# A two-block transformer kernel: expert slots weighted one at a time on ScalarE, choices in pieces, gathered rows also in the weight ring

## The chip, the core and the metric

The kernel runs on one core of a Trainium2 chip. The metric is the device time of one execution in microseconds (us); before is the median of three runs. Engines are named as the profile names them: PE (matmul), PEld (weight load), DVE (VectorE), ACT (ScalarE), POOL (GpSimd) and SP (which issues most loads).

## The reference

256 tokens of width 1024 pass through a first block (two layers of feed-forward, three attention-like branches and feed-forward) and a second block of two layers. Each layer of the second block is a mixer of five groups and then an expert layer, and only the expert layer is touched here:

```python
def peer_ffn(xn, wq, subkeys, u_tab, v_tab):
    q = (xn @ wq).reshape(b, s, PEER_HEADS, 2, PEER_HALF)
    sc = jnp.einsum('bshjc,hjkc->bshjk', q, subkeys)
    top_s, top_i = lax.top_k(sc, PEER_TOPK)
    ...                        # best 16 of the sums of both halves -> idx; g = softmax(best)
        act = jax.nn.gelu(jnp.einsum('ckd,cd->ck', u_tab[ic], xc), approximate=False)
        return jnp.einsum('ck,ckd->cd', (gc * act).astype(v_tab.dtype), v_tab[ic])
```

The table of experts has 16,384 rows per layer; a row holds u (1024 floats) and v (1024 floats) side by side, 8 KB. A token uses 8 x 16 = 128 of them, so a tile of 128 tokens needs 128 gathers ("slots"), each of 128 rows, 1 MB (1.049 million bytes); the two tiles of a layer need 256 slots, and both layers 512.

## The kernel before, in words

Everything is 32-bit. The first block and the mixers stream weights from memory through a ring of three 1 MB buffers (`raw`), which ACT and DVE (or POOL) split into a high and a low part (`hi` L212, `lo` L216) for three matmuls per product (`mm3`, L236). SP issues these loads as the ring comes free.

The expert layer is `peer`. `arrive` finishes a tile's input, `project(h)` computes the queries of a head (one 1 MB weight unit, 48 matmuls of L236) and the scores of its keys, and `route(tt, h)` chooses the 16 experts of a head on DVE (some 45 small instructions) and writes their numbers to `idx` and their softmax to `gate`. Then `experts` goes through the slots in groups of GROUP = 4:

- four times: POOL gathers a slot's rows into one of GBUFS = 8 buffers `uv` (L1377, an indirect DMA); DVE multiplies the u half with the token and sums it into one column of `act` (the "dot", L1379);
- once for the four: ACT takes Gelu of the 128x4 `act` (L1383), DVE multiplies it with the gates (L1384);
- four times: ACT scales the identity with one column (`dgw`, L1387), and PE multiplies that diagonal with the v half of the row (L1389: two halves of 512 columns, each recorded as two MATMULs), summing all 128 slots of a tile in `p_y`.

So a buffer `uv` is free for the next gather only when PE has read it, which is behind the dot of the last slot of its group.

What runs beside the slots is in `todo`: steps with the slot from which they may be issued. `issue_after(dots[-1])` ties a step behind the last dot of the group before; a whole `project` or `route` is one step. Tile 0 carries six projections, the second tile's arrival and the choices of its later heads, tile 1 the choices of its heads alone. The order of instructions within each engine is made at build time by a scheduler with a model of the time; the engines then run their lists in order, and semaphores hold them. Behind tile 0 the ring `raw` is free, and SP fills it with the first weights of the next mixer (`win2_s`); in the last layer it stays empty.

The changed function, with the line numbers of the profile:

Of the kernel before, what the change touches and what calls it, by code (L numbers as in the profile page):

```python
# [8 lines left out]
F32 = mybir.dt.float32  # L9
# [4 lines left out]
AF = mybir.ActivationFunctionType  # L14
OP = mybir.AluOpType
# [3 lines left out]
P = 128  # L19
T = 256  # L20
D = 1024
L = 2
NT = T // P
# [7 lines left out]
HEADS = 8  # L31
TOPK = 16
# [11 lines left out]
NEXP = NKEYS * NKEYS  # L44

GBUFS = 8
XG_AT = 3
GROUP = 4
NB2 = 17
LO = 4  # L50
BANKS = {"mm": 2, "acc": 4, "tr": 2}
# [124 lines left out]
class _Kernel:  # L176
# [1069 lines left out]
    def peer(self, l, x, xt, y_in):  # L1246
# [9 lines left out]
        def arrive(tt):  # L1256


            ss = self.small.tile([P, 2], F32, tag="rms_s", name="rms_s")
            r = rs[tt] = self.small.tile([P, 1], F32, tag="rms_r", name="rms_r", bufs=NT)  # L1260
            for i in range(2):
                sl = slice(512 * i, 512 * i + 512)
                nc.vector.tensor_tensor(x[tt][:, sl], y_in[tt][i], x[tt][:, sl], op=OP.add)
                nc.vector.tensor_tensor(xg[tt][:, sl], x[tt][:, sl], self.gain[:, sl], op=OP.mult)
                self.transposed(xg[tt][:, sl], KT // 2, xt, tt, k0=i * KT // 2)
            for i in range(2):
                sl = slice(512 * i, 512 * i + 512)
# [53 lines left out]
        def route(tt, h):  # L1321

            small = lambda n, t=F32, k=TOPK: W.tile([P, k], t, tag=n, name=n, bufs=2)
            sc = scores[tt, h]
            tv = W.tile([P, 2, TOPK], F32, tag="tv", name="tv", bufs=2)
            ti = W.tile([P, 2, TOPK], U32, tag="ti", name="ti", bufs=2)
            for j in range(2):
                top16(sc[:, j], tv[:, j], ti[:, j])

            c = W.tile([P, NPAIRS], F32, tag="cand", name="cand", bufs=2)  # L1330
            for a0, a1, w, at in PAIRS:
                nc.vector.tensor_tensor(c[:, at:at + (a1 - a0) * w].rearrange("p (a b) -> p a b", b=w),
                                        tv[:, 0, a0:a1].unsqueeze(2).to_broadcast([P, a1 - a0, w]),
                                        tv[:, 1, :w].unsqueeze(1).to_broadcast([P, a1 - a0, w]), op=OP.add)
            best, ci = small("best"), small("ci", U32)
            top16(c, best, ci)
            ids = W.tile([P, 2, TOPK], F32, tag="ids", name="ids", bufs=2)
            nc.vector.tensor_copy(ids, ti)

            cf, ai, ab, i1, i2 = small("cf"), small("ai", I32), small("ab"), small("i1"), small("i2")  # L1340
            nc.vector.tensor_copy(cf, ci)
            nc.vector.tensor_scalar(i1, cf, -11.5, 1.0 / 8.0, op0=OP.add, op1=OP.mult)
            nc.vector.tensor_scalar(i2, cf, -29.0, 1.0 / 3.0, op0=OP.add, op1=OP.mult)
            nc.vector.scalar_tensor_tensor(ai, i1, 0.0, i2, op0=OP.max, op1=OP.max)
            nc.vector.tensor_copy(ab, ai)
            nc.vector.tensor_scalar(i1, ab, 8.0, 8.0, op0=OP.mult, op1=OP.add)
            nc.vector.tensor_scalar(i2, ab, 3.0, 28.0, op0=OP.mult, op1=OP.add)
            nc.vector.scalar_tensor_tensor(i1, ab, 16.0, i1, op0=OP.mult, op1=OP.min)
            nc.vector.tensor_tensor(i1, i1, i2, op=OP.min)
            nc.vector.tensor_tensor(cf, cf, i1, op=OP.subtract)  # L1350
            for j, (pos, out) in enumerate(((ab, i1), (cf, i2))):
                e = W.tile([P, TOPK, TOPK], F32, tag="eq", name="eq", bufs=2)
                nc.vector.tensor_tensor(e, pos.unsqueeze(2).to_broadcast([P, TOPK, TOPK]),
                                        self.iota[:, :TOPK].unsqueeze(1).to_broadcast([P, TOPK, TOPK]), op=OP.is_equal)
                nc.vector.tensor_tensor(e, e, ids[:, j].unsqueeze(1).to_broadcast([P, TOPK, TOPK]), op=OP.mult)
                nc.vector.tensor_reduce(out, e, axis=AX.X, op=OP.add)
            nc.vector.scalar_tensor_tensor(i1, i1, float(NKEYS), i2, op0=OP.mult, op1=OP.add)
            last = nc.vector.tensor_scalar(idx[:, tt, h], i1, float(l * NEXP), None, op0=OP.add)
# [12 lines left out]
        def experts(tt, h, k0):

            rows = []
            act = W.tile([P, GROUP], F32, tag="act", name="act", bufs=3)
            for i in range(GROUP):
                r = uv.pop(0) if uv else W.tile([P, 2 * D], F32, tag="uv", name="uv", bufs=GBUFS)
                nc.gpsimd.indirect_dma_start(out=r, out_offset=None, in_=a["puv"],  # L1377
                                             in_offset=bass.IndirectOffsetOnAxis(ap=idx[:, tt, h, k0 + i:k0 + i + 1], axis=0))
                dots.append(nc.vector.scalar_tensor_tensor(r[:, :D], r[:, :D], 1.0, xg[tt], op0=OP.mult, op1=OP.mult,  # L1379
                                                           accum_out=act[:, i:i + 1]))  # L1380
                rows.append(r)
            wt = W.tile([P, GROUP], F32, tag="wt", name="wt", bufs=3)
            nc.scalar.activation(wt, act, AF.Gelu, scale=rs[tt])  # L1383
            nc.vector.tensor_tensor(wt, wt, gate[:, tt, h, k0:k0 + GROUP], op=OP.mult)  # L1384
            for i, r in enumerate(rows):
                dg = W.tile([P, P], F32, tag="dgw", name="dgw", bufs=4)
                nc.scalar.activation(dg, self.ident, AF.Copy, scale=wt[:, i:i + 1])  # L1387
                for half in range(2):
                    nc.tensor.matmul(y[tt][half], dg, r[:, D + 512 * half:D + 512 * half + 512],  # L1389
                                     start=h == 0 and k0 + i == 0, stop=h == HEADS - 1 and k0 + i == TOPK - 1)  # L1390


        weights(0)
        arrive(0)
        project(0, 0, 1)
        dots = [route(0, 0)]
        weights(1)
        project(1, 0, 1)

        def late():  # L1400
            arrive(1)
            if l + 1 < L:
                self.load_gain(l + 1)
            project(0, 1)
            project(1, 1)


        todo = [(0, lambda: route(0, 1)), (GROUP, late)]
        for h in range(2, HEADS):
            todo += [(TOPK * h - 22, lambda h=h: project(h)), (TOPK * h - 14, lambda h=h: route(0, h))]  # L1410
        for h in range(HEADS):
            todo.append((TOPK * (HEADS + h) - 24, lambda h=h: route(1, h)))
        todo.sort(key=lambda t: t[0])
        for n, (tt, h) in enumerate([(tt, h) for tt in range(NT) for h in range(HEADS)]):
            for k0 in range(0, TOPK, GROUP):
                while todo and todo[0][0] <= TOPK * n + k0:
                    step = todo.pop(0)[1]
                    with self.tc.issue_after(dots[-1].ins):
                        step()
                experts(tt, h, k0)  # L1420
        assert not todo
        return y

# [54 lines left out]
```

## Time and profile before

| | us |
|---|---|
| median of 3 runs (lowest, highest) | 3249.17 (3243.63, 3259.98) |
| the profiled execution | 3238.84 |
| its span, first to last instruction | 3237.1 |
| expert layer 0, first gather issued to last matmul | 1606.9 to 2347.7: 740.8 |
| expert layer 1, the same | 2515.0 to 3233.2: 718.2 |

The profile is of one execution; its span is 1.7 us under that execution's time, and that time 10.3 us under the median of the runs. A "stage" below is one tile of an expert layer; the four are 1606.9 to 1986, 1986 to 2347.7, 2515 to 2879 and 2879 to 3233.2 us. An engine's list is in order, so an idle time is read with what ended it (the text behind `<-`).

### The profile page before, as it was taken

What the parts mean: (1) busy time and instruction counts of PE and PEld (TensorE: products, weight loads), DVE (VectorE), ACT (ScalarE), POOL (GpSimd) and SP (SyncE); (2) the same over time, 40 slices, a digit from 0 to 9 for tenths busy, and PEclk for the clock granted to TensorE, in tenths of its full rate; (3) what the DMA queues carried; (4) which work ended last, traced back from release to release, by engine and by line L of the source; (5) the groups of instructions that cost most, each with busy time, mean ns of one, the idle gap of its engine ahead of it and who ended that gap; (6) DMA issues with size and microseconds to landing.
All of it is one profiled execution on the core that took longest, in us unless ns stands there. A gap on an engine that the chain in (4) does not pass through costs nothing.

```text
span 3237.1 us, 39712 instructions
## 1 busy us (share of the span) xinstructions
PE 2814.0 (87%) x13968; PEld 2058.1 (64%) x13968; DVE 2131.9 (66%) x4974; ACT 1199.3 (37%) x2300; POOL 882.7 (27%) x628
## 2 busy tenths in 40 slices
PE   9999999999999999999788877777889688867777
PEld 9988988989988988978644433332377344323333
DVE  6568667565577567569766676666487666766664
ACT  5446344445445344436432222212164322222121
POOL 0013221011023220011234454434311444444343
PEclk9999999999999999999889988888899899898889
DMA  6554235555553344554399999999843899999998
GB/s 256 183 187 158 100 122 202 183 182 213 182 189 135 105 156 176 182 184 144 129 379 397 391 371 365 397 378 374 344 146 108 347 391 376 378 399 384 379 376 353
DMA packets 121734, 841.78 MB, mean 260 GB/s; under 512 B 14016, under 2 KB 16832, under 8 KB 22208
## 3 DMA queue, kind: packets, MB, share of 16 engines
q0 software_dynamic: 73728, 536.90, 41.4%
q1 hardware_dynamic: 47520, 301.82, 26.2%
q8 instruction: 111, 1.82, 0.2%
q14 instruction: 87, 0.71, 0.1%
q10 hardware_dynamic: 288, 0.52, 0.0%
HBM read 838.15 MB, written 1.05 MB: 259 GB/s over the span
## 4 chain that ended last, share of the span: by engine, by line
PE 46%; DMA 19%; DVE 17%; issue 9%; POOL 6%; ACT 2%; POOLq 0%; DVEq 0%; SPq 0%; ACTq 0%
DMA uv<-in_puv_dram,idx 19%; PE p_gu L236 14%; PE p_y L236 10%; POOL uv L1377 6%; DVE uv L1379 4%; PE p_g L236 4%; PE p_y L1389 3%; PE p_b L236 2%; PE p_c L236 2%; PE p_gx L236 2%; DVE conv L542 1%; DVE lo L216 1%; PE p_tr L293 1%; PE p_s L236 1%; ACT hi L212 1%
## 5 line engine op out<-in xcount | busy, mean ns | idle before, releaser
L1389 PE MATMUL p_y<-uv,dgw 128*128 128x512 f32 x2048 | 1024.9, 659 | 295.8 <-ACT dgw L1387 295.8
L1389 PEld LDWEIGHTS p_y<-uv,dgw 128*128 128x128 f32 x2048 | 423.5, 212 | 866.5 <-issue 498.8
L1379 DVE SCALAR_TENSOR_TENSOR uv<-uv,xg 128x1024 f32<-128x1024 f32 x512 | 632.6, 1237 | 479.4 <-DMA uv<-in_puv_dram,idx 448.4
L1377 POOL DMA_INDIRECT uv<-in_puv_dram,idx x512 | 603.1, 1178 | 870.9 <-PE p_y L1389 508.3
L216 DVE TENSOR_TENSOR lo<-raw,hi 128x1024 fp32r<-128x1024 f32 (+1 forms) x390 | 480.7, 1236 | 311.9 <-ACT hi L212 309.9
L212 ACT CAST hi<-raw 128x1024 fp32r<-128x1024 f32 (+1 forms) x500 | 513.8, 1034 | 449.4 <-PE p_gu L236 125.1
L216 POOL TENSOR_TENSOR lo<-raw,hi 128x1024 fp32r<-128x1024 f32 (+1 forms) x110 | 274.4, 2500 | 1446.6 <-ACT hi L212 860.1
L236 PE MATMUL p_gu<-xt,hi 128*128 128x256 f32 x2560 | 463.6, 283 | 0.0
L236 PEld LDWEIGHTS p_gu<-xt,hi 128*128 128x128 f32 x2560 | 399.6, 192 | 0.0
L236 PE MATMUL p_gu<-xt,lo 128*128 128x256 f32 x1280 | 362.5, 283 | 0.0
L1383 ACT ACTIVATE wt<-act,rms_r 128x4 f32<-128x4 f32 x128 | 38.1, 297 | 848.2 <-DVE uv L1379 848.1
L236 PEld LDWEIGHTS p_gu<-xt,lo 128*128 128x128 f32 x1280 | 245.7, 192 | 0.0
L1387 ACT ACTIVATE dgw<-ident,wt 128x128 f32<-128x128 f32 x512 | 165.6, 391 | 77.6 <-DVE wt L1384 65.3
L236 PE MATMUL p_c<-xt,hi 128*128 128x256 f32 x960 | 182.6, 290 | 0.4 <-ACT sh L1095 0.4
L236 PE MATMUL p_y<-hi,ht 128*128 128x512 f32 x576 | 181.2, 395 | 0.0
L236 PEld LDWEIGHTS p_c<-xt,hi 128*128 128x128 f32 x960 | 152.9, 194 | 2.4 <-ACT sh L1095 1.1
L236 PE MATMUL p_c<-xt,lo 128*128 128x256 f32 x480 | 138.2, 289 | 0.0
L236 PE MATMUL p_y<-lo,ht 128*128 128x512 f32 x320 | 126.3, 395 | 0.0
L236 PE MATMUL p_g<-hi,xt 128*128 128x512 f32 x384 | 125.1, 399 | 0.0
L236 PEld LDWEIGHTS p_y<-hi,ht 128*128 128x128 f32 x576 | 108.5, 188 | 25.1
L236 PEld LDWEIGHTS p_c<-xt,lo 128*128 128x128 f32 x480 | 92.9, 194 | 0.2
L236 PE MATMUL p_g<-lo,xt 128*128 128x512 f32 x192 | 77.3, 403 | 8.2 <-DVE lo L216 7.0
(517 smaller groups left out, 3953.0 us busy)
## 6 DMA issues: line engine op xcount, KB each, us to landing
raw<-in_gu_dram SPq DMA_DIRECT2D x86, 1024.0 KB, 4.8
raw<-in_dn_dram SPq DMA_DIRECT2D x44, 1024.0 KB, 4.8
raw<-in_win_t_dram SPq DMA_DIRECT2D x30, 1024.0 KB, 4.9
raw<-in_win_g_dram SPq DMA_DIRECT2D x24, 1024.0 KB, 4.8
raw<-in_wout_dram SPq DMA_DIRECT2D x18, 1024.0 KB, 4.9
raw<-in_wq_dram SPq DMA_DIRECT2D x16, 1024.0 KB, 4.9
raw<-in_wbr_dram SPq DMA_DIRECT2D x12, 1024.0 KB, 4.8
raw<-in_win_s_dram SPq DMA_DIRECT2D x8, 1024.0 KB, 8.1
```

Of the source, the lines that this page charges most:

```text
L212: self.nc.scalar.copy(hi, r)
L216: engine.tensor_tensor(lo[:, a:b], r[:, a:b], hi[:, a:b].bitcast(F32), op=OP.subtract)
L236: self.nc.tensor.matmul(out, A[i], B[j], start=first and n == 0, stop=last and n == 2)
L293: nc.tensor.transpose(p[:, j], x[:, (g + j) * P:(g + j + 1) * P], self.ident)
L542: nc.vector.scalar_tensor_tensor(c[:, s:], th[:, j, :T - s], pc[:, 4 * f + 3 - s:4 * f + 4 - s], c[:, s:], op0=OP.mult, op1=OP.add)
L1377: nc.gpsimd.indirect_dma_start(out=r, out_offset=None, in_=a["puv"], in_offset=bass.IndirectOffsetOnAxis(ap=idx[:, tt, h, k0 + i:k0 + i + ...
L1379: dots.append(nc.vector.scalar_tensor_tensor(r[:, :D], r[:, :D], 1.0, xg[tt], op0=OP.mult, op1=OP.mult, accum_out=act[:, i:i + 1]))
L1383: nc.scalar.activation(wt, act, AF.Gelu, scale=rs[tt])
L1387: nc.scalar.activation(dg, self.ident, AF.Copy, scale=wt[:, i:i + 1])
L1389: nc.tensor.matmul(y[tt][half], dg, r[:, D + 512 * half:D + 512 * half + 512], start=h == 0 and k0 + i == 0, stop=h == HEADS - 1 and k0 + ...
```

## The change

Slots are weighted one by one: Gelu of a 128x1 `act`, then the gate as a second ACT instruction (a copy scaled by the gate's column), then `dgw`; the multiply of four gates on DVE is gone. `arrive`, `route` and the projections become generators; `beside` issues one piece of them behind the dot of each slot whose number has reached the step's, until the step is done, and ties the piece behind that dot. Routes of tile 1 begin at slot 128 + 16h - 20 instead of 128 + 16h - 24. The second head's choice of tile 0 is issued at once, ahead of the slots. In tile 1 three slots of every eleven go to a buffer of the weight ring (`raw`) instead of `uv`, in layer 0 up to slot 107, in layer 1 to the end. Of the diff, the removal of the constant GROUP (which moves lines up by one) and the repeated yields are cut:

```diff
@@ arrive: one piece per half, then the rest
                 self.transposed(xg[tt][:, sl], KT // 2, xt, tt, k0=i * KT // 2)
+                yield
...
@@ route: a yield behind each top16, behind the candidates, behind the decoding and between the two look-ups
             for j in range(2):
                 top16(sc[:, j], tv[:, j], ti[:, j])
+                yield
...
             top16(c, best, ci)
+            yield
...
-            last = nc.vector.tensor_scalar(idx[:, tt, h], i1, float(l * NEXP), None, op0=OP.add)
+            chosen = nc.vector.tensor_scalar(idx[:, tt, h], i1, float(l * NEXP), None, op0=OP.add)
+            if not dots:
+                dots.append(chosen)
...
-        def experts(tt, h, k0):
-            rows = []
-            act = W.tile([P, GROUP], F32, tag="act", name="act", bufs=3)
-            for i in range(GROUP):
-                r = uv.pop(0) if uv else W.tile([P, 2 * D], F32, tag="uv", name="uv", bufs=GBUFS)
-                nc.gpsimd.indirect_dma_start(out=r, out_offset=None, in_=a["puv"],
-                                             in_offset=bass.IndirectOffsetOnAxis(ap=idx[:, tt, h, k0 + i:k0 + i + 1], axis=0))
-                dots.append(nc.vector.scalar_tensor_tensor(r[:, :D], r[:, :D], 1.0, xg[tt], op0=OP.mult, op1=OP.mult,
-                                                           accum_out=act[:, i:i + 1]))
-                rows.append(r)
-            wt = W.tile([P, GROUP], F32, tag="wt", name="wt", bufs=3)
+        def expert(tt, h, k):
+            n = TOPK * h + k
+            if uv:
+                r = uv.pop(0)
+            elif tt == NT - 1 and n % 11 in (0, 4, 7) and n < (108 if l + 1 < L else 128):
+                r = self.ring.tile([P, 2 * D], F32, tag="raw", name="raw", bufs=3)
+            else:
+                r = W.tile([P, 2 * D], F32, tag="uv", name="uv", bufs=GBUFS)
+            nc.gpsimd.indirect_dma_start(out=r, out_offset=None, in_=a["puv"],
+                                         in_offset=bass.IndirectOffsetOnAxis(ap=idx[:, tt, h, k:k + 1], axis=0))
+            act, wt = [W.tile([P, 1], F32, tag=nm, name=nm, bufs=4) for nm in ("act", "wt")]
+            dot = nc.vector.scalar_tensor_tensor(r[:, :D], r[:, :D], 1.0, xg[tt], op0=OP.mult, op1=OP.mult, accum_out=act)
+            dots.append(dot)
+            beside(dot)
             nc.scalar.activation(wt, act, AF.Gelu, scale=rs[tt])
-            nc.vector.tensor_tensor(wt, wt, gate[:, tt, h, k0:k0 + GROUP], op=OP.mult)
-            for i, r in enumerate(rows):
-                dg = W.tile([P, P], F32, tag="dgw", name="dgw", bufs=4)
-                nc.scalar.activation(dg, self.ident, AF.Copy, scale=wt[:, i:i + 1])
-                for half in range(2):
-                    nc.tensor.matmul(y[tt][half], dg, r[:, D + 512 * half:D + 512 * half + 512],
-                                     start=h == 0 and k0 + i == 0, stop=h == HEADS - 1 and k0 + i == TOPK - 1)
+            nc.scalar.activation(wt, wt, AF.Copy, scale=gate[:, tt, h, k:k + 1])
+            dg = W.tile([P, P], F32, tag="dgw", name="dgw", bufs=4)
+            nc.scalar.activation(dg, self.ident, AF.Copy, scale=wt)
+            for half in range(2):
+                nc.tensor.matmul(y[tt][half], dg, r[:, D + 512 * half:D + 512 * half + 512],
+                                 start=n == 0, stop=n == HEADS * TOPK - 1)
+        def at_once(steps):
+            for _ in steps:
+                pass
+        dots = []
         weights(0)
-        arrive(0)
+        at_once(arrive(0))
         project(0, 0, 1)
-        dots = [route(0, 0)]
+        at_once(route(0, 0))
         weights(1)
         project(1, 0, 1)
+        with self.tc.issue_after(dots[0].ins):
+            at_once(route(0, 1))
         def late():
-            arrive(1)
+            yield from arrive(1)
             if l + 1 < L:
                 self.load_gain(l + 1)
-            project(0, 1)
-            project(1, 1)
-        todo = [(0, lambda: route(0, 1)), (GROUP, late)]
+            for h in range(2):
+                yield
+                project(h, 1)
+        def ahead(h):
+            project(h)
+            yield
+        todo = [(3, late())]
         for h in range(2, HEADS):
-            todo += [(TOPK * h - 22, lambda h=h: project(h)), (TOPK * h - 14, lambda h=h: route(0, h))]
+            todo += [(TOPK * h - 22, ahead(h)), (TOPK * h - 14, route(0, h))]
         for h in range(HEADS):
-            todo.append((TOPK * (HEADS + h) - 24, lambda h=h: route(1, h)))
+            todo.append((TOPK * (HEADS + h) - 20, route(1, h)))
         todo.sort(key=lambda t: t[0])
-        for n, (tt, h) in enumerate([(tt, h) for tt in range(NT) for h in range(HEADS)]):
-            for k0 in range(0, TOPK, GROUP):
-                while todo and todo[0][0] <= TOPK * n + k0:
-                    step = todo.pop(0)[1]
-                    with self.tc.issue_after(dots[-1].ins):
-                        step()
-                experts(tt, h, k0)
+        def beside(dot):
+            if todo and todo[0][0] <= len(dots) - 2:
+                with self.tc.issue_after(dot.ins):
+                    while todo and next(todo[0][1], todo) is todo:
+                        todo.pop(0)
+                        if not todo or todo[0][0] > len(dots) - 2:
+                            break
+        for tt in range(NT):
+            for h in range(HEADS):
+                for k in range(TOPK):
+                    expert(tt, h, k)
         assert not todo
         return y
```

What the scheduler makes of it is seen in the lists of the engines. The first place is ACT in tile 0 of layer 0, one group of four slots and the work of a projection behind it (`wt` is the weight of the slots, `dgw` the diagonal, `hi` a split of the next weights, `q` and `sc` a head's query and scores). Before:

```order
L1383 ACTIVATE wt<-act,rms_r 128x4
L1387 ACTIVATE dgw<-ident,wt 128x128 x4
L212 CAST hi<-raw 128x1024 x2
L1307 COPY q<-p_q 128x512
L1286 ACTIVATE sc<-p_sc,rms_r 128x256 x2
```

and now:

```order
L1393 ACTIVATE wt<-act,rms_r 128x1
L1394 ACTIVATE wt<-wt,gate_15631 128x1
L1396 ACTIVATE dgw<-ident,wt 128x128
L211 CAST hi<-raw 128x1024 x2
L1307 COPY q<-p_q 128x512
```

One Gelu and four diagonals have become three instructions for every slot, and the casts and copies stand between single slots. The number of table loads on ACT is the same in both lists, 66.

The second place is DVE in tile 0 of layer 0, the end of a head's choice (`eq` looks up the expert numbers, `idx` takes them). Before:

```order
L1379 SCALAR_TENSOR_TENSOR uv,act<-uv,xg_15635 128x1024
L1355 TENSOR_TENSOR eq<-eq,ids 128x256
L1356 TENSOR_REDUCE i_16258<-eq 128x16
L1384 TENSOR_TENSOR wt<-wt,gate_15631 128x4
L1357 SCALAR_TENSOR_TENSOR i_16257<-i_16257,i_16258 128x16
L1358 TENSOR_SCALAR idx<-i_16257 128x16
L1379 SCALAR_TENSOR_TENSOR uv,act<-uv,xg_15635 128x1024 x4
L216 TENSOR_TENSOR lo<-raw,hi 128x1024 x2
L1384 TENSOR_TENSOR wt<-wt,gate_15631 128x4
```

and now:

```order
L1390 SCALAR_TENSOR_TENSOR uv,act<-uv,xg_15635 128x1024
L1356 TENSOR_TENSOR eq<-cf,iota 128x256
L1370 TENSOR_SCALAR pm<-best 128x1
L1358 TENSOR_TENSOR eq<-eq,ids 128x256
L1359 TENSOR_REDUCE i_17249<-eq 128x16
L1372 RECIPROCAL pz<-pz 128x1
L1362 SCALAR_TENSOR_TENSOR i_17248<-i_17248,i_17249 128x16
L1373 TENSOR_SCALAR gate_15631<-gate_15631,pz 128x16
L1363 TENSOR_SCALAR idx<-i_17248 128x16
L1390 SCALAR_TENSOR_TENSOR uv,act<-uv,xg_15635 128x1024 x3
L215 TENSOR_TENSOR lo<-raw,hi 128x1024 x2
```

The multiply `wt`, which stood among the dots and waits for ACT, is gone; a piece of the choice stands behind one dot, the two splits `lo` behind the third dot after it.

The third place is POOL in layer 0, all its gathers (`uv` or `raw` is the buffer) with the splits `lo` of the next mixer's weights among them. Before:

```order
L1377 DMA uv<-in_puv_dram,idx 128x2048 x96
L216 TENSOR_TENSOR lo<-raw,hi 128x1024 x2
L1377 DMA uv<-in_puv_dram,idx 128x2048 x4
L216 TENSOR_TENSOR lo<-raw,hi 128x1024 x2
L1377 DMA uv<-in_puv_dram,idx 128x2048 x156
```

and now, first the beginning of tile 1, then the end of it:

```order
L1387 DMA uv<-in_puv_dram,idx 128x2048 x121
L1387 DMA raw<-in_puv_dram,idx 128x2048 x3
L1387 DMA uv<-in_puv_dram,idx 128x2048 x15
L1387 DMA raw<-in_puv_dram,idx 128x2048
L1387 DMA uv<-in_puv_dram,idx 128x2048 x3
```

```order
L1387 DMA uv<-in_puv_dram,idx 128x2048 x10
L215 TENSOR_TENSOR lo<-raw,hi 128x1024
L1387 DMA uv<-in_puv_dram,idx 128x2048
L215 TENSOR_TENSOR lo<-raw,hi 128x1024
L1387 DMA uv<-in_puv_dram,idx 128x2048 x2
L215 TENSOR_TENSOR lo<-raw,hi 128x1024
L1387 DMA uv<-in_puv_dram,idx 128x2048
L215 TENSOR_TENSOR lo<-raw,hi 128x1024
L1387 DMA uv<-in_puv_dram,idx 128x2048 x7
```

The first three ring slots of tile 1 are gathered seven slots early (behind gather 120 instead of 127), and the four splits of the next mixer's weights, which stood in tile 0 behind gathers 95 and 99, now stand among the last eleven gathers of tile 1.

## Rows read from the trace of the kernel before

**Rows 1.** The page: rate of the DMAs in 40 slices; the chain that ended last.
```profile
GB/s 256 183 187 158 100 122 202 183 182 213 182 189 135 105 156 176 182 184 144 129 379 397 391 371 365 397 378 374 344 146 108 347 391 376 378 399 384 379 376 353
...
DMA uv<-in_puv_dram,idx 19%; PE p_gu L236 14%; PE p_y L236 10%; POOL uv L1377 6%; DVE uv L1379 4%; PE p_g L236 4%; PE p_y L1389 3%; PE p_b L236 2%; PE p_c L236 2%; PE p_gx L236 2%; DVE conv L542 1%; DVE lo L216 1%; PE p_tr L293 1%; PE p_s L236 1%; ACT hi L212 1%
```
**Rows 2.** Windows, four stages: us; busy of PE, PEld, DVE, ACT, POOL; clock; DMA.
```profile
1606.90:1986.00 379.10, 298.36 (x896) 153.18 (x897) 254.37 (x755) 103.36 (x237) 166.62 (x134) 0.88 0.95 381
1986.00:2347.70 361.70, 278.02 (x565) 117.54 (x563) 214.24 (x600) 72.83 (x195) 145.44 (x127) 0.87 0.93 371
2515.00:2879.00 364.00, 286.19 (x899) 149.12 (x900) 247.05 (x755) 99.16 (x234) 157.99 (x131) 0.91 0.96 382
2879.00:3233.20 354.20, 263.78 (x530) 109.32 (x528) 210.09 (x586) 70.02 (x188) 142.51 (x126) 0.89 0.94 379
```
**Rows 3.** The gathers' line L1377: duration, why POOL was idle, time to landing.
```profile
L1377 POOL DMA_INDIRECT uv<-in_puv_dram,idx x512: 932/938/1988, 1607.0 to 3213.8; - x171
...
  PE p_y L1389: 508.3, 311
...
DMA to landing us min/median/max: 5.5/9.1/15.2
```
**Rows 4.** Timeline of a group of four slots in layer 1, tile 1.
```profile
2968.45 1.23 DVE L1379 SCALAR_TENSOR_TENSOR uv<-uv,xg 128x1024 f32<-128x1024 f32 x1 [2.47 <-DMA uv<-in_puv_dram,idx]
...
2976.99 1.23 DVE L1379 SCALAR_TENSOR_TENSOR uv<-uv,xg 128x1024 f32<-128x1024 f32 x1 [1.26 <-DMA uv<-in_puv_dram,idx]
...
2978.26 0.30 ACT L1383 ACTIVATE wt<-act,rms_r 128x4 f32<-128x4 f32 x1 [9.69 <-DVE uv L1379]
2978.59 0.16 DVE L1384 TENSOR_TENSOR wt<-wt,gate 128x4 f32<-128x4 f32 x1 [0.36 <-ACT wt L1383]
2979.12 1.28 ACT L1387 ACTIVATE dgw<-ident,wt 128x128 f32<-128x128 f32 x4 [0.57 <-DVE wt L1384]
...
2979.58 8.83 PE L1389 MATMUL p_y<-uv,dgw 128*128 128x512 f32 x16 [4.64 <-ACT dgw L1387]
...
2983.08 0.94 POOL L1377 DMA_INDIRECT uv<-in_puv_dram,idx  x1 [6.55 <-PE p_y L1389]
...
2989.17 0.94 POOL L1377 DMA_INDIRECT uv<-in_puv_dram,idx  x1 [0.31 <-DVE cand L1332]
```
**Rows 5.** Timeline near the end of layer 1: two dots, with one left out between.
```profile
3213.91 1.23 DVE L1379 SCALAR_TENSOR_TENSOR uv<-uv,xg 128x1024 f32<-128x1024 f32 x1 [1.22 <-DMA uv<-in_puv_dram,idx]
...
3218.80 1.23 DVE L1379 SCALAR_TENSOR_TENSOR uv<-uv,xg 128x1024 f32<-128x1024 f32 x1 [1.22 <-DMA uv<-in_puv_dram,idx]
```
**Rows 6.** Windows of 40 us, the one with the highest rate.
```profile
3160.00:3200.00 40.00, 30.46 (x68) 12.59 (x68) 19.99 (x35) 6.30 (x20) 17.54 (x17) 0.99 1.01 426
```
**Rows 7.** Windows, the slots' matmuls L1389 alone, last stage: PE, PEld, clock, DMA.
```profile
2879.00:3233.20 354.20, 263.78 (x530) 109.32 (x528) 0.89 0.94 379
```
**Rows 8.** Windows, the weight matmuls L236 alone, first stage.
```profile
1606.90:1986.00 379.10, 48.05 (x336) 42.18 (x336) 0.88 0.95 381
```
**Rows 9.** Timeline of PE, the slots' matmuls after three idle times.
```profile
2946.76 7.13 PE L1389 MATMUL p_y<-uv,dgw 128*128 128x512 f32 x16 [2.38 <-ACT dgw L1387]
2958.82 16.11 PE L1389 MATMUL p_y<-uv,dgw 128*128 128x512 f32 x32 [4.93 <-ACT dgw L1387]
...
2989.34 7.13 PE L1389 MATMUL p_y<-uv,dgw 128*128 128x512 f32 x16 [0.93 <-ACT dgw L1387]
```
**Rows 10.** ACT by line, 1990 to 2330 us: busy, mean ns, idle before.
```profile
L1387 ACT ACTIVATE dgw<-ident,wt 128x128 f32<-128x128 f32 x120 | 39.0, 391 | 14.6 <-DVE wt L1384 10.8 <-PE p_y L1389 3.8
L1383 ACT ACTIVATE wt<-act,rms_r 128x4 f32<-128x4 f32 x31 | 9.2, 298 | 225.8 <-DVE uv L1379 225.8
```
**Rows 11.** Timeline of POOL at the start of layer 0's slots: gathers 8 and 9.
```profile
1616.86 1.69 POOL L1377 DMA_INDIRECT uv<-in_puv_dram,idx  x1 [0.30 <-issue]
1628.96 0.94 POOL L1377 DMA_INDIRECT uv<-in_puv_dram,idx  x1 [10.40 <-DVE rms_r L284]
```
**Rows 12.** The page, group of POOL's splits.
```profile
L216 POOL TENSOR_TENSOR lo<-raw,hi 128x1024 fp32r<-128x1024 f32 (+1 forms) x110 | 274.4, 2500 | 1446.6 <-ACT hi L212 860.1
```

More of the change, by code (lines that the diff above doesn't have):

```diff
@@ L47 @@
 XG_AT = 3
-GROUP = 4
 NB2 = 17
@@ L1356, in route @@
                 nc.vector.tensor_reduce(out, e, axis=AX.X, op=OP.add)
+                if j == 0:
+                    yield
             nc.vector.scalar_tensor_tensor(i1, i1, float(NKEYS), i2, op0=OP.mult, op1=OP.add)
-            last = nc.vector.tensor_scalar(idx[:, tt, h], i1, float(l * NEXP), None, op0=OP.add)
+            chosen = nc.vector.tensor_scalar(idx[:, tt, h], i1, float(l * NEXP), None, op0=OP.add)
+            if not dots:
+                dots.append(chosen)
             z = small("pz", k=1)
@@ L1366, in route @@
             nc.vector.tensor_scalar(g, g, z, None, op0=OP.mult)
-            return last
         y = [[self.bank([512], "acc", "p_y") for _ in range(2)] for _ in range(NT)]
-        def experts(tt, h, k0):
-            rows = []
-            act = W.tile([P, GROUP], F32, tag="act", name="act", bufs=3)
-            for i in range(GROUP):
-                r = uv.pop(0) if uv else W.tile([P, 2 * D], F32, tag="uv", name="uv", bufs=GBUFS)
-                nc.gpsimd.indirect_dma_start(out=r, out_offset=None, in_=a["puv"],
-                                             in_offset=bass.IndirectOffsetOnAxis(ap=idx[:, tt, h, k0 + i:k0 + i + 1], axis=0))
-                dots.append(nc.vector.scalar_tensor_tensor(r[:, :D], r[:, :D], 1.0, xg[tt], op0=OP.mult, op1=OP.mult,
-                                                           accum_out=act[:, i:i + 1]))
-                rows.append(r)
-            wt = W.tile([P, GROUP], F32, tag="wt", name="wt", bufs=3)
-            nc.scalar.activation(wt, act, AF.Gelu, scale=rs[tt])
-            nc.vector.tensor_tensor(wt, wt, gate[:, tt, h, k0:k0 + GROUP], op=OP.mult)
-            for i, r in enumerate(rows):
-                dg = W.tile([P, P], F32, tag="dgw", name="dgw", bufs=4)
-                nc.scalar.activation(dg, self.ident, AF.Copy, scale=wt[:, i:i + 1])
-                for half in range(2):
-                    nc.tensor.matmul(y[tt][half], dg, r[:, D + 512 * half:D + 512 * half + 512],
-                                     start=h == 0 and k0 + i == 0, stop=h == HEADS - 1 and k0 + i == TOPK - 1)
@@ L1408, in peer @@
-        todo = [(0, lambda: route(0, 1)), (GROUP, late)]
+            for h in range(2):
+                yield
+                project(h, 1)
+        def ahead(h):
+            project(h)
+            yield
+        todo = [(3, late())]
         for h in range(2, HEADS):
-            todo += [(TOPK * h - 22, lambda h=h: project(h)), (TOPK * h - 14, lambda h=h: route(0, h))]
+            todo += [(TOPK * h - 22, ahead(h)), (TOPK * h - 14, route(0, h))]
         for h in range(HEADS):
-            todo.append((TOPK * (HEADS + h) - 24, lambda h=h: route(1, h)))
+            todo.append((TOPK * (HEADS + h) - 20, route(1, h)))
```

## The prediction, made before the changed kernel was run

> **What bounds the kernel now.** I read the page first, then the windows of the four expert stages, then the gathers' line, then one group of slots in the timeline. The slices show two stretches with the DMAs near 380 GB/s and everything else far below; they are the expert layers, and the longest entry of the chain of waits is their gathers' landing [rows 1]. The stages last 379.1 + 361.7 + 364.0 + 354.2 = 1459 us, 45% of the span, for 512 slots: 2.85 us a slot. No compute engine is full there: PE is busy 74 to 79%, DVE 59 to 68%, ACT 20 to 27% [rows 2].
>
> The DMAs are the nearest to full, but they are not the bound by themselves. Where two dots follow landings the pace is (3218.80 - 3213.91) / 2 = 2.445 us a slot [rows 5], which is 1.049 MB / 2.445 us = 429 GB/s; the best window has 426 [rows 6], the stages only 371 to 382 [rows 2]. What is missing is gathers in flight. POOL stood idle 508.3 us until PE had read a buffer [rows 3]. In the group of rows 4 the first slot's row has landed at 2968.45, waits for three more dots, one Gelu, the gates and PE, and its buffer is taken again at 2983.08: 14.6 us. The fourth slot's takes 2976.99 to 2989.17: 12.2 us. The mean of 13.4 us held plus the median 9.1 us from issue to landing [rows 3] is 22.5 us, and eight buffers at that stage's 354.2 / 128 = 2.77 us make 22.1. So the eight buffers set the pace, by the time that a group of four holds them.
>
> **The change part by part.** *Weights slot by slot.* A buffer's hold becomes its dot (1.23 us [rows 4]), one Gelu (0.30 [rows 10]), the gate on ACT, one diagonal (0.39 [rows 10]), three or four hand-overs of about 0.3 us, and PE: four MATMULs, a quarter of 7.13 us = 1.78 us [rows 9], then POOL's reaction. The gate's ACT instruction isn't in the trace; from below it is the 0.16 us of the DVE multiply it replaces [rows 4], from above a diagonal, 0.39; I take the Gelu's 0.30, as the nearest in shape and engine. Sum 1.2 + 0.3 + 0.3 + 0.4 + 1.2 + 1.8 + 0.5 = 5.7 us, against 13.4. Eight buffers then leave 8 x 2.45 - 5.7 = 13.9 us for the flight, which has a median of 9.1 now: the buffers no longer set the pace, the DMAs do. It would take a hold of over 8 x 2.45 - 9.1 = 10.5 us to bring the old bound back.
>
> ACT gains 384 Gelus and 512 gates, 896 x 0.30 = 269 us, onto 345 busy in the stages [rows 2]: 614 of 1459, still idle most of the time. Each slot waits twice on ACT behind its own instructions; queued behind it are the casts, `q` copies and scores of a projection and the softmax of a choice, which PE and DVE need sixteen slots later, so they cost nothing while ACT has that idle time. DVE loses 128 multiplies of 0.16 us = 20 us and its wait for ACT in the middle of the dots; nothing is late for it.
>
> *The floor.* Bytes of a stage are its time by its rate; at 429 GB/s the stages would need 144.4 MB -> 337, 134.2 -> 313, 139.0 -> 324 and 134.2 -> 313 us. To that I add 4 us at the start of each layer (first gather to the DMAs being busy) and 5 us at its end (one slot's chain where four stood): 341, 318, 328, 318. Against rows 2 that is 38 + 44 + 36 + 36 = 154 us at most.
>
> *How much of it.* Tile 1 has little beside the slots: PE's slots take 263.8 / 128 = 2.06 us each [rows 7], under 2.45, and that includes the slow start of each burst; DVE has 210 us for 313. I take 85% there: 68 us. Tile 0 also carries the projections (48 us of PE, about 6.9 us for each of seven [rows 8]), the weights' splits on DVE and casts on ACT, all in order in front of some slot: PE 298 us and DVE 254 [rows 2], plus gaps between dependent small instructions, for 341. A slot behind a projection is held 5.7 + 6.9 = 12.6 us, over the 10.5, so for two or three slots in sixteen the queue runs thin. I take 55%: 40 us. Together 108 us.
>
> *Start of a layer.* Now the eighth gather is issued at 1616.86 and the ninth at 1628.96, after 10.4 idle us, since four dots and a group stand before the first release [rows 11]. One slot's chain ends at about 1607 (the first gather) + 5.5 (the shortest landing [rows 3]) + 5.7 = 1618, so this gap goes; it is within tile 0's share.
>
> *Pieces behind single dots.* The instructions of a choice stay the same, and DVE ran them between dots already. Numbers come in time: the last piece stands behind dot 16h - 9 and the gather of slot 16h waits for the buffer of 16h - 8. Value nothing; if one comes a piece late, POOL stands some 2 us, at 30 heads at most 60 us, which only the wide range holds.
>
> *Rows in the weight ring.* Three more buffers in tile 1 allow a hold of 11 x 2.45 - 9.1 = 17.9 us; with 5.7 held they are cover for something already covered, so nothing. They cost order: the first three are gathered seven slots early, which moves 7.3 us of transfers ahead of slots with eight in flight; and layer 0's next weights are loaded and split among the last twenty slots instead of earlier. POOL's four splits of 2.5 us each [rows 12] stand among eleven gathers, which take 27 us at the floor's pace: room enough. If the next mixer finds its weights late, one ring refill of three loads, 3 x 2.45 = 7 us, once; I take 0 of 0 to 7.
>
> So 3238.84 - 108 = 3131 us for an execution like the profiled one; the median of the runs lies 10.3 us above it, so I predict 3249 - 108 = 3141.
>
> **The rivals.** *The DMA floor is reached everywhere:* -154, 3249 - 154 = 3095. For it: PE and DVE are under 90% of the floor even in tile 0. Against: in-order queues with pieces of 7 us.
>
> *Tile 0 doesn't move:* ACT, PE and DVE each wait for the other in order there, three ACT instructions a slot among casts; then only tile 1's 68 us, 3181.
>
> *Nothing moves,* since the DMAs are at their limit already: their busy share is 0.93 to 0.96 [rows 2]. Then about 3249. Against it stands 426 GB/s over 40 us [rows 6], 12% above the stages' rate. The Trainium skill (DMA: Bandwidth & Descriptors, Specifications) states a limit of some 358 GB/s from memory for one core; by it a slot could not be under 2.93 us and the stages would already be past the limit, so here the trace overrules it. The same table's ceiling of 435 GB/s at the SBUF side fits the 429.
>
> *PE's clock falls and it is slower.* The slots' PE work comes in bursts of 7 to 16 us now, and the granted clock is 0.87 to 0.91 in the stages [rows 2], the mean of its two levels, 2.4 and 1.2 GHz. A burst after 4.93 idle us took 16.11 for eight slots; after 0.93 and 2.38 idle it took 7.13 for four, so 14.26 for eight [rows 9]: the first lost 1.85 at the lower level. One slot at a time leaves 2.45 - 1.78 = 0.67 us idle, shorter than either, so I expect the clock to hold. If it doesn't: PE's work of 512 x 1.78 + 2 x 48 = 1007 us grows to 1007 (1 + s) with a share s of it at the lower level, and exceeds the 1459 us of now from s = 0.45. At s = 0.55 it is 1561 us: +102, 3351. The Trainium skill (TensorE: Matmul & The Clock Gate, A second HAM failure mode: psum-queue depth-cycling) says that frequent short idles between groups of matmuls make the clock swing between its levels; the row after 0.93 us doesn't agree.
>
> **How the numbers follow.** The forecast (3115 to 3165) 0.50; the floor 0.20; tile 1 alone 0.17; nothing 0.08; slower 0.05. Below 3090 and above 3205 I leave out some 0.17, so the range is 3090 to 3205. About 0.5%, 16 us, is what a measurement of this kernel tells from no change: faster 0.87, same 0.08, slower 0.05.
>
> **What would show it.** After the change POOL's wait for PE should fall from 508 us to under 200, the time from issue to landing should rise to 11 to 16 us (more in flight), DVE should wait for landings at single paces of 2.45 us, and the DMAs should show over 410 GB/s in tile 1's windows. The ramp's 10.4 us should be gone. ACT should be busy some 270 us longer. I am wrong in the step on holds if flight stays near 9 us with POOL still waiting for PE; in the floor if flight grows and the rate doesn't pass 390; in tile 0 if its stages stay above 365 us with PE or ACT as the releaser; and about the clock if it is granted under 0.8 in tile 1.

## The result, and the profile after

The changed kernel takes 3109.38 us (median of 4 runs, 3106.2 to 3112.98) against 3246.66 us for the kernel before on the same chip (3243.63 to 3259.98): a ratio of 0.957, 95% interval 0.954 to 0.960. That is 137 us less, where 108 were forecast; 3109 lies in the range of 3090 to 3205, between the forecast of 3141 and the rival in which the DMA floor is reached everywhere (3095). It is 6 us below the band of 3115 to 3165 that had the chance of 0.50, and nearer to the rival than to the forecast.

The page of the kernel after has the same two stretches as [rows 1], now flat: the DMAs move 420 to 427 GB/s in the slices inside them, where they moved 344 to 399.

```profile
DMA  7544325555555334555249999999952699999998
GB/s 263 179 171 173 116 88 197 203 191 197 188 175 175 111 109 163 197 184 211 82 172 424 427 424 427 426 427 427 422 215 82 254 426 425 420 427 427 427 427 347
...
PE 49%; DMA 23%; DVE 19%; issue 4%; ACT 3%; POOL 2%; POOLq 0%; SPq 0%; DVEq 0%; ACTq 0%
```

The four stages follow as windows of the kernel after, with the columns of [rows 2]: length, busy time of PE, PEld, DVE, ACT and POOL, granted clock, share and rate of the DMAs.

```profile
1614.70:1960.60 345.90, 289.73 (x917) 144.09 (x918) 250.24 (x712) 169.68 (x462) 156.95 (x138) 0.95 1.01 422
1960.60:2283.20 322.60, 253.85 (x545) 95.51 (x543) 221.06 (x578) 150.88 (x419) 160.28 (x122) 0.99 0.98 411
2450.50:2795.50 345.00, 289.92 (x917) 145.02 (x918) 250.47 (x712) 169.56 (x461) 156.18 (x138) 0.95 1.01 421
2795.50:3107.30 311.80, 250.36 (x513) 91.73 (x511) 210.83 (x565) 145.48 (x408) 149.36 (x118) 0.98 0.97 410
```

The border between the tiles is here the last slot's matmul of tile 0. In [rows 2] it was set some 8 us earlier, in the middle of a burst of PE; by the rule used here the windows of the kernel before are these:

```profile
1606.90:1994.80 387.90, 307.16 (x916) 156.78 (x916) 257.69 (x761) 104.82 (x242) 172.27 (x139) 0.88 0.95 381
1994.80:2347.60 352.80, 269.21 (x545) 113.93 (x544) 210.87 (x593) 71.26 (x191) 139.79 (x121) 0.86 0.93 370
2515.00:2886.60 371.60, 293.79 (x916) 152.15 (x916) 249.51 (x759) 100.28 (x237) 162.47 (x135) 0.92 0.96 382
2886.60:3233.10 346.50, 256.13 (x513) 106.28 (x512) 207.61 (x581) 68.90 (x184) 138.03 (x122) 0.89 0.94 379
```

The sum falls from 1458.8 to 1325.3 us: -133.5, of it -42, -30, -27 and -35 in the four stages. Between the layers nothing was gained: from the end of layer 0's slots to the first gather of layer 1 it is 167.3 us in both. The profiled execution gained 3238.84 - 3112.98 = 125.9 us, 7.6 less than its stages, because its first gather was issued at 1614.7 instead of 1606.9; in the traces of the runs below that moment lies between 1608.8 and 1613.7. Why it wanders was not tried.

Within a stage the slots now go in lock-step with the landings. Timeline of the kernel after near the end of layer 1 (start, duration, engine, line and operation, in brackets the idle time before and what ended it):

```profile
3092.16 1.22 DVE L1390 SCALAR_TENSOR_TENSOR uv<-uv,xg 128x1024 f32<-128x1024 f32 x1 [1.21 <-ACT dgw L1396]
...
3093.43 0.29 ACT L1393 ACTIVATE wt<-act,rms_r 128x1 f32<-128x1 f32 x1 [1.39 <-DVE uv L1390]
3093.76 0.29 ACT L1394 ACTIVATE wt<-wt,gate 128x1 f32<-128x1 f32 x1
3094.08 0.40 ACT L1396 ACTIVATE dgw<-ident,wt 128x128 f32<-128x128 f32 x1
...
3094.54 1.98 PE L1398 MATMUL p_y<-uv,dgw 128*128 128x512 f32 x4 [0.46 <-ACT dgw L1396]
3094.60 1.23 DVE L1390 SCALAR_TENSOR_TENSOR uv<-uv,xg 128x1024 f32<-128x1024 f32 x1 [1.21 <-ACT dgw L1396]
```

From the start of the dot at 3092.16 to the end of PE at 3096.52 a row is held 4.36 us; in [rows 4] it was 14.6 and 12.2, counted to the buffer's next gather. The dots stand 2.44 us apart, each behind half a slot's idle time: every engine waits for the DMAs. The dot's releaser is put down to `dgw`, but that ACT instruction ended at 3092.04, 2.46 us after the one of the slot before: it follows the dots' pace and doesn't set it.

### The profile page after: what moved, and what is told of

Its sections match the earlier page's. It is cut to its first block, busy times and chain, and to the rows that moved or that the text cites. A ratio compares the mean times of both kernels' runs of the same rounds, so it can differ in the third digit from the quotient of the medians.

```text
span 3111.2 us, 40472 instructions
## 1 busy us (share of the span) xinstructions
PE 2777.6 (89%) x13968; PEld 2009.9 (65%) x13968; DVE 2140.4 (69%) x4846; ACT 1490.1 (48%) x3196; POOL 891.8 (29%) x628
## 3 DMA queue, kind: packets, MB, share of 16 engines
q1 hardware_dynamic: 47520, 301.82, 27.3%
## 4 chain that ended last, share of the span: by engine, by line
PE 49%; DMA 23%; DVE 19%; issue 4%; ACT 3%; POOL 2%; POOLq 0%; SPq 0%; DVEq 0%; ACTq 0%
DMA uv<-in_puv_dram,idx 19%; PE p_gu L235 15%; PE p_y L235 10%; DVE uv L1390 5%; PE p_g L235 4%; DMA raw<-in_puv_dram,idx 3%; PE p_y L1398 3%; PE p_b L235 2%; PE p_c L235 2%; POOL uv L1387 2%; PE p_gx L235 2%; PE p_s L235 1%; DVE conv L541 1%; DVE lo L215 1%; PE p_q L235 1%
## 5 line engine op out<-in xcount | busy, mean ns | idle before, releaser
L1398 PE MATMUL p_y<-uv,dgw 128*128 128x512 f32 x1788 | 867.1, 622 | 221.1 <-ACT dgw L1396 204.7
L1398 PEld LDWEIGHTS p_y<-uv,dgw 128*128 128x128 f32 x1788 | 325.2, 194 | 716.1 <-ACT dgw L1396 416.6
L1390 DVE SCALAR_TENSOR_TENSOR uv<-uv,xg 128x1024 f32<-128x1024 f32 x447 | 550.1, 1237 | 292.2 <-DMA uv<-in_puv_dram,idx 164.1
L1387 POOL DMA_INDIRECT uv<-in_puv_dram,idx x447 | 529.6, 1185 | 654.8 <-PE p_y L1398 272.9
L1393 ACT ACTIVATE wt<-act,rms_r 128x1 f32<-128x1 f32 x512 | 150.2, 293 | 569.3 <-DVE uv L1390 483.9
L1396 ACT ACTIVATE dgw<-ident,wt 128x128 f32<-128x128 f32 x512 | 205.1, 401 | 15.1
L1394 ACT ACTIVATE wt<-wt,gate 128x1 f32<-128x1 f32 x512 | 150.6, 294 | 16.0
L1398 PE MATMUL p_y<-raw,dgw 128*128 128x512 f32 x260 | 129.2, 620 | 31.0 <-ACT dgw L1396 30.9
```

What stands on the lines that cost most here:

```text
L1390: dot = nc.vector.scalar_tensor_tensor(r[:, :D], r[:, :D], 1.0, xg[tt], op0=OP.mult, op1=OP.mult, accum_out=act)
L1394: nc.scalar.activation(wt, wt, AF.Copy, scale=gate[:, tt, h, k:k + 1])
L1396: nc.scalar.activation(dg, self.ident, AF.Copy, scale=wt)
```

## The experiments

My theory: a buffer is held for h us and a row is in flight for f us, so eight buffers allow a slot every (h + f) / 8 us; below 2.45 us the DMAs' rate takes over and f grows until the sum fits. The rivals: the choices in pieces or the ring's rows bring the gain; the gain is in proportion to what leaves the hold; the pace is a cost per gather and not one of bytes. Holds below run from the start of a slot's dot to the end of its last matmul, averaged over a tile. So counted, the kernel before holds a buffer for 13.3, 12.2, 12.7 and 11.9 us in its four stages, the kernel after for 6.3, 4.9, 6.5 and 4.8.

The trace of the kernel after gives no landings. What it gives is the time from a gather's issue to the start of its dot, which is the flight and the wait for DVE's turn. Averaged over a tile, that was 9.4 to 9.9 us before; it is 13.9 and 13.7 after in tile 0, 20 in tile 1 with its eleven buffers, and 13.3 to 15.0 in the kernel after without the ring's rows. So the rows do queue longer where the hold is short.

**One slot at a time, and nothing else.** In the kernel before:

```diff
-GROUP = 4
+GROUP = 1
```

> The kernel before with GROUP = 1 and nothing else: gate on DVE, whole steps, no rows in the ring. Theory: the hold falls just as with the change, so nearly all of the gain comes, 3105 to 3135 us. Rival (the gate's move to ACT, or the pieces tied behind single dots, is what makes the difference): less than a third of the 137 us, over 3200 us.

Measured: 3114.38 us (3111.87 to 3117.08), ratio 0.9612 [0.9584, 0.9641]; stages 353.0, 319.7, 338.6 and 321.1, sum 1332.4; hold 5.8, 4.7, 6.2 and 4.5 us. One constant brings nearly all of it. For the gate on ACT, the pieces and the ring's rows together some 5 us are left, and the intervals of the two ratios overlap. With GROUP = 1 the steps of `todo` are also issued between single slots, though each step still whole; that part wasn't separated.

**After, without the ring's rows.**

```diff
-            elif tt == NT - 1 and n % 11 in (0, 4, 7) and n < (108 if l + 1 < L else 128):
+            elif False:
```

> The changed kernel with every row in one of the eight buffers uv, none in the weight ring. Theory (the time a buffer is held set the pace; one slot at a time shortens the hold from 13.4 us to about 5.7, so eight buffers are enough): the same as the changed kernel within 0.4%, 3100 to 3120 us, tile 1's stages at 312 to 328 us and about 425 GB/s. Rival (the three extra buffers are what fills the DMAs in tile 1): tile 1's stages go back to 345 us or more each, 3150 us or more.

Measured: 3110.55 us (3109.26 to 3114.82), ratio 0.9607 [0.9578, 0.9637]; stages 350.9, 318.8, 337.6 and 319.5, sum 1326.8 against 1325.3. Nothing, as predicted: layer 0 takes 669.7 us without the ring's rows and 668.5 with them, layer 1 657.1 and 656.8. In layer 1 one sees three gathers change the tile, 3 x 2.45 = 7.4 us: with the ring's rows tile 0 is 7.4 longer and tile 1 7.7 shorter. Layer 0 doesn't show it: there tile 0 is 5.1 shorter, after a first gather 5.9 later, and tile 1 3.9 longer. Part of why three more buffers are of no use is in the list of POOL's instructions with their waits (the last two gathers of the kernel after):

```
L1387 DMA uv<-in_puv_dram,idx 128x2048 [waits DMASW6_49,DVE_49,PE_49]
L1387 DMA uv<-in_puv_dram,idx 128x2048 [waits DMASW7_49,DVE_49,PE_49]
```

The gathers take eight completion semaphores in turn, DMASW0 to DMASW7, and each waits for the last user of its own; in the trace, too, eight semaphores serve 64 of the 512 gathers each. So no more than eight should be in flight, however many buffers there are, and the 20 us from issue to dot in tile 1 are, at 2.45 us a slot, some eight rows. In the kernel after POOL then waits for landings, which the kernel before did not show as a releaser [rows 3]; its gathers, with durations and releasers:

```profile
L1387 POOL DMA_INDIRECT uv<-in_puv_dram,idx x447: 935/960/2003, 1614.7 to 3083.0; - x149
L1387 POOL DMA_INDIRECT raw<-in_puv_dram,idx x65: 939/1372/1992, 1919.9 to 3078.1; - x65
its engine sat idle before it (us, times) until:
  PE p_y L1398: 281.5, 171
  DMA uv<-in_puv_dram,idx: 74.8, 68
...
  DMA raw<-in_puv_dram,idx: 40.5, 30
```

**The ring's rows alone, with groups of four.** The kernel before, in its loop over a group:

```diff
-                r = uv.pop(0) if uv else W.tile([P, 2 * D], F32, tag="uv", name="uv", bufs=GBUFS)
+                n = TOPK * h + k0 + i
+                ring = tt == NT - 1 and n % 11 in (0, 4, 7) and n < (108 if l + 1 < L else 128)
+                r = (uv.pop(0) if uv else self.ring.tile([P, 2 * D], F32, tag="raw", name="raw", bufs=3) if ring
+                     else W.tile([P, 2 * D], F32, tag="uv", name="uv", bufs=GBUFS))
```

> The kernel before, groups of four kept, with three of every eleven rows of tile 1 in the weight ring (eleven buffers). Theory: 13.4 us held + 9.1 us in flight over 11 buffers is 2.05 us a slot, under the DMAs' 2.45, so tile 1's stages come to the floor, 316 to 330 us instead of 362 and 354, tile 0 stays at 379 and 364: 3160 to 3185 us. Rival (the groups' bursts on PE, which start at the lower clock after an idle time, set the pace, not the buffers): tile 1 stays above 345 us, 3225 us or more.

Measured: 3191.62 us (3185.43 to 3198.35), ratio 0.9856 [0.9822, 0.989]. Windows of its four stages, same columns:

```profile
1612.80:1999.00 386.20, 298.23 (x916) 153.56 (x916) 260.06 (x811) 103.74 (x241) 166.87 (x138) 0.89 0.96 379
1999.00:2325.40 326.40, 260.92 (x544) 111.21 (x544) 208.99 (x543) 72.68 (x191) 144.82 (x122) 0.90 0.97 405
2489.70:2872.60 382.90, 299.55 (x916) 154.27 (x916) 260.64 (x811) 103.21 (x241) 157.35 (x138) 0.89 0.96 382
2872.60:3184.10 311.50, 246.34 (x512) 102.50 (x512) 196.26 (x530) 66.23 (x180) 133.57 (x118) 0.93 0.97 408
```

Tile 1 goes from 370 and 379 GB/s to 405 and 408 with its hold hardly changed at 12.6 and 11.8 us: more buffers do there what a shorter hold does. Tile 0 stays at 379 and 382. The total came out 7 us above the expected 3160 to 3185. Three gathers more go into tile 0, and in layer 1 it grew from 371.6 to 382.9 us; but in layer 0, with the same three, it didn't (387.9 and 386.2), so that these gathers cost the 7 us is not shown. In tile 1 both parts of the change cure the same shortage, and whichever comes second is worth nothing.

**Five buffers with the short hold.** The kernel after without the ring's rows, and:

```diff
-GBUFS = 8
+GBUFS = 5
```

> The changed kernel without rows in the ring and with five buffers uv instead of eight. Theory, by the accounts of a buffer: 5.7 us held + 1 us of issue + 5.5 us of the shortest flight is 12.2 us, over five buffers 2.44 us a slot, just the floor, with no slack for a projection: tile 1 at 318 to 340 us, tile 0 at 350 to 385, 3120 to 3185 us. Rival (a flight takes its 9 us whatever the queue): 14.8 / 5 = 2.96 us a slot, all stages near 379 us, 3290 us or more.

Measured: 3237.27 us (3232.34 to 3242.09), ratio 0.9989 [0.9974, 1.0004]: the time of the kernel before, and between the two expectations, so both were off. Its gathers, from issue to landing:

```profile
  PE p_y L1398: 580.9, 312
...
DMA to landing us min/median/max: 6.2/8.0/11.9
```

With a hold of 4.7 us in the last stage and the prediction's 0.5 us for POOL's reaction, (4.7 + 8.0 + 0.5) / 5 = 2.64 us, against 348.9 / 128 = 2.73 measured. The account holds to 3%, with landings of only 64 of the 512 gathers in this trace; I had put in a flight of 5.5 us, and 8.0 was measured. Five buffers held for 5 us are worth eight held for 13.

This run also settles a rival that I had not named, that the gain came from the clock, which rose with the change. With five buffers the granted clock is 0.95 to 0.97 in all four stages, against 0.86 to 0.92 in the kernel before, and their sum is 1457.0 us against 1458.8. The last stage:

```profile
2881.60:3230.50 348.90, 262.04 (x513) 93.09 (x512) 212.06 (x562) 146.43 (x411) 131.32 (x124) 0.96 0.96 378
```

**Groups of two.** The kernel before:

```diff
-GROUP = 4
+GROUP = 2
```

> The kernel before with groups of two slots instead of four, nothing else. My theory (eight buffers, held and in flight, against 2.45 us of transfer a slot): a group of two holds a buffer for about 7 us in tile 1 and 8 in tile 0, under the 10.5 at which the buffers set the pace again, so the stages come to the floor as with single slots: 320 +- 6 us in tile 1, 350 +- 10 in tile 0, total 3105 to 3135. Rival: the gain is proportional to what leaves the hold, so groups of two bring about two thirds of what single slots bring: stages near 1375 us in sum, total 3150 to 3170.

Measured: 3118.35 us (3117.9 to 3120.52), ratio 0.9593 [0.9577, 0.9609]; stages 354.4, 320.2, 341.4 and 322.7, sum 1338.7; hold 8.2, 6.9, 8.2 and 6.6 us. Its gathers:

```profile
  PE p_y L1389: 399.0, 238
  DVE uv L1379: 162.3, 126
...
DMA to landing us min/median/max: 5.4/12.3/15.9
```

This is a threshold and no proportion: a hold of 7 to 8 us gives what 5 to 6 gives, within 7 us of the sum of single slots, while 12 to 13 costs 120 us more. Where between 8 and 12 us the threshold lies was not measured; the 10.5 of the prediction is an estimate. The median flight grew from 9.1 [rows 3] to 12.3 us, and (6.9 + 12.3 + 0.5) / 8 = 2.46 us, with the same reaction, is the pace of the floor. POOL still waits 399 us for PE, at the floor.

**Half the bytes.** The kernel after without the ring's rows, and each gather fetches 4 KB a partition, which serve as both halves:

```diff
-            nc.gpsimd.indirect_dma_start(out=r, out_offset=None, in_=a["puv"],
+            nc.gpsimd.indirect_dma_start(out=r[:, D:], out_offset=None, in_=a["puv"].rearrange("n (t d) -> (n t) d", t=2),
...
-            dot = nc.vector.scalar_tensor_tensor(r[:, :D], r[:, :D], 1.0, xg[tt], op0=OP.mult, op1=OP.mult, accum_out=act)
+            dot = nc.vector.scalar_tensor_tensor(r[:, :D], r[:, D:], 1.0, xg[tt], op0=OP.mult, op1=OP.mult, accum_out=act)
```

> The kernel after without the ring rows, and each gather fetches 4 KB a partition instead of 8 (one half of the row serves as both, so the output is another one). My theory (after the change the bytes set the pace, PE is next with 1.98 us a slot): tile 1 falls from 2.45-2.5 to 2.0-2.2 us a slot, stages of 260 to 285 us, tile 0 to 290 to 325, PE over 90% busy in the stages, total 2900 to 2990. Rival: the pace of 2.45 us is one of gathers (POOL's work for each, or a cost per row), not of bytes: the stages stay within 3%, total 3070 to 3115.

Measured: 2853.89 us (2851.63 to 2856.15), ratio 0.878 [0.8762, 0.8797], below what I expected. Its stages:

```profile
1613.40:1919.60 306.20, 279.76 (x917) 146.18 (x918) 241.09 (x698) 165.77 (x466) 173.80 (x139) 0.95 0.75 261
1919.60:2155.60 236.00, 229.16 (x544) 100.96 (x542) 203.63 (x592) 130.47 (x414) 151.05 (x121) 1.00 0.79 273
2319.80:2618.90 299.10, 278.81 (x917) 145.34 (x918) 236.55 (x707) 161.73 (x465) 160.71 (x135) 0.97 0.72 248
2618.90:2850.40 231.50, 224.90 (x512) 96.17 (x511) 198.46 (x570) 126.87 (x404) 161.34 (x121) 0.99 0.82 281
```

So bytes set the pace after the change, and not the number of gathers: 512 gathers of 128 rows take 1072.8 us instead of 1326.8. PE is next, busy 97% in tile 1 at 231.5 / 128 = 1.81 us a slot. I had taken the 1.98 us of a slot by itself; back to back a slot costs less.

## Why the prediction was right, and where it was off

- **The bound, and what lifts it: right.** Eight buffers at the hold of a group of four set the pace before, the DMAs after. One constant alone shows it, and five buffers with the short hold restore the old time, at the higher clock.
- **The hold: right in the mean.** I took 5.7 us, 5.2 without POOL's reaction; the averages are 6.3 and 6.5 in tile 0, 4.9 and 4.8 in tile 1. The gate took 0.29 us where 0.30 was taken. The hand-overs were the part that was off: four of 0.3 us were put in, and in the timeline above they are 0.05, 0.04, 0.03 and 0.06. PE's slot is 1.98 us and not 1.78: it now stands alone, and 1.78 was a quarter of four that overlap. So an undisturbed slot takes 4.36 us and not 5.2; the means came near 5.2 only because waits that the sum doesn't hold, most of them in tile 0, made up the difference. That is luck.
- **The floor of 429 GB/s: right.** Most windows of 40 us inside the stages show 424 to 427.
- **How much of it: the step that was off.** I took 85% of the possible gain in tile 1 and 55% in tile 0. By the borders used here, and with the floor worked out as before from the bytes (348.5, 309, 335 and 311 us), the kernel after without ring rows reaches 71 of 76 us in tile 0 (93%) and 61 of 79 in tile 1 (77%): 132 against 108. Tile 1 gave 7 less than forecast and tile 0 31 more. Tile 1's shortfall lies at its two ends, as three windows of layer 0 show, without ring rows:

```profile
1959.70:1999.70 40.00, 35.31 (x94) 17.38 (x94) 30.77 (x93) 20.37 (x57) 16.87 (x16) 0.96 0.94 371
1999.70:2039.70 40.00, 30.79 (x65) 10.89 (x64) 28.17 (x81) 18.70 (x52) 15.73 (x16) 1.00 1.01 427
2268.50:2278.50 10.00, 8.09 (x17) 2.71 (x16) 4.40 (x8) 3.66 (x12) 0.00 (x0) 1.00 0.17 70
```

  Against 429 GB/s the first loses 5.4 us; DVE does the last steps of tile 0 there among the dots (whether they are the cause was not tried). The last loses 8.4, where 5 were put in for the end of a layer. By this estimate the two make 8.8 of the 9.7 us by which that stage misses its floor. In tile 0 I had argued that a slot held over 10.5 us behind a projection lets the queue run thin. Such slots are there: in the kernel after seven of tile 0 in layer 0 are held over 10.5 us, the longest, whose dot is at 1740.9, 11.4. The window with that slot does not show it:

```profile
1694.70:1734.70 40.00, 34.52 (x116) 17.47 (x115) 28.36 (x81) 20.16 (x53) 18.08 (x16) 0.97 1.01 426
1734.70:1774.70 40.00, 35.30 (x118) 18.25 (x117) 28.37 (x80) 19.88 (x53) 17.18 (x16) 0.97 1.01 426
```

  The threshold is one for the mean and not for a single slot. At a mean hold of 6 us I estimate that (8 x 2.45 - 6) / 2.45 = 5.5 rows stand in the queue, some 13.6 us of transfers, and that a slot that is 5 us late is paid from that stock.
- **Ring rows and pieces at nothing: right.** For the ring's rows two runs show it. The pieces were not run by themselves, and could have gained what the gate on ACT lost, or the other way; together the two make 4 us between single slots alone and the kernel after without ring rows (3114.38 and 3110.55).
- **The start of a layer: right.** The ninth gather follows 1.13 us of idle time after the eighth, against 10.40 in [rows 11]:

```profile
1624.47 1.69 POOL L1387 DMA_INDIRECT uv<-in_puv_dram,idx  x1 [0.30 <-issue]
1627.30 1.22 POOL L1387 DMA_INDIRECT uv<-in_puv_dram,idx  x1 [1.13 <-PE p_y L1398]
```

- **ACT's 270 us: 290, and free as argued.** The three lines of ACT in the kernel after (busy, mean ns of one):

```profile
L1396 ACT ACTIVATE dgw<-ident,wt 128x128 f32<-128x128 f32 x512 | 205.1, 401 | 15.1
L1394 ACT ACTIVATE wt<-wt,gate 128x1 f32<-128x1 f32 x512 | 150.6, 294 | 16.0
L1393 ACT ACTIVATE wt<-act,rms_r 128x1 f32<-128x1 f32 x512 | 150.2, 293 | 569.3 <-DVE uv L1390 483.9 <-DVE raw L1390 74.5 <-issue 2.7
```

  Gelus and gates came to 150.2 + 150.6 - 38.1 = 263 us more (38.1 is L1383 in the kernel before), near the 269 of the prediction. The other 27 us are lost overlap, which I had left out: four diagonals in a row overlapped, 39.0 / 120 = 0.325 us each in [rows 10], and alone one takes 0.401. ACT stood idle 483.9 + 74.5 = 558 us until a dot was done.
- **POOL's wait for PE under 200 us: wrong as a sign.** It is 281.5 us in the kernel after, 462.0 without ring rows and 399.0 with groups of two, all at the floor. When the DMAs are the bound, the buffers are all taken too, and the last thing that POOL waits for is still PE's release. Flight and rate tell the two cases apart, not the releaser. The flight did lengthen as predicted, to 12.3 us with groups of two; in the kernel after the time from issue to dot shows it.
- **The clock: right, and to the good side.** It was not lowered by the short pauses of 0.47 us between slots; it rose from between 0.86 and 0.92 in the stages to between 0.95 and 0.99, and PE's busy time in them fell from 1126 to 1084 us. The rule of the Trainium skill that I weighed (TensorE: Matmul & The Clock Gate, A second HAM failure mode: psum-queue depth-cycling) would have made this kernel slower; here the trace, with 0.95 to 0.99, disagrees with it. What went before a lower clock in [rows 9] is a longer pause between groups of four, of 4.93 us.

## What to carry to other kernels

Where a stage streams rows through N buffers, work out (hold + flight) / N from the trace and set it against the pace of the transfers by themselves; what shortens the hold and what adds buffers are the same cure, and past the threshold either is worth nothing more. Count the hold from the first row of a batch, since batching held four buffers to save a few instructions of 0.3 us on an engine that was idle. A late slot counts only against the stock in the queue, though several in a row can empty it, and "waits for the release of a buffer" does not tell a shortage of buffers from a full pipe: look at flight and rate.

## What the runs showed of the hardware that was not expected

At the floor one DMA engine seems to fall behind the others. The DMAs in the last stretch of the kernel after, 3092 to 3104 us in 40 equal parts:

```profile
DMA  9999997755432111000000000000010000000000
GB/s 437 437 437 410 437 410 328 300 246 246 191 137 109 82 55 55 27 27 27 27 27 27 27 27 27 27 27 27 27 27 0 0 27 27 0 0 0 0 0 0
```

437 / 16 = 27.3: for some 5 us the rate is that of a single engine of sixteen (the view doesn't tell the engines apart), and the last dot waits for it (2.17 us idle before the dot at 3102.93). The same stretch of the kernel before falls from 291 GB/s to nothing within 1.4 us (with five buffers, too, it goes in steps of 0.45 us from 437 over 346 and 109 to nothing, while single slots alone and the kernel after without ring rows end with the long tail):

```profile
GB/s 382 473 400 437 437 382 492 364 437 437 401 401 455 400 473 291 127 36 0 0 0 0 0 0 0 0 0 0 0 0 0 0 0 0 0 0 0 0 0 0
```

The Trainium skill (DMA: Bandwidth & Descriptors, Latency and other measured facts) says that two of the sixteen engines are usually slower than the rest in such transfers; the trace agrees with one laggard here and does not name it. Its cause was not tried.

The second thing is the sustained rate, with one core at work: 420 to 427 GB/s over slices of 78 us inside the stages, and 410 to 422 over whole stages with their ends. The Trainium skill (DMA: Bandwidth & Descriptors, Bandwidth) gives some 358, the limit that the prediction quoted, for two cores that stream at once; no run here shows that case.
